# Part of a modulation product in a two-block transformer kernel, moved from VectorE to TensorE

## The chip, the core and the metric

The kernel runs on one core of a Trainium2 chip. The metric is the device time of one execution in microseconds. TensorE is PE in the rows of the profile (its weight loads are listed apart, as PEld), VectorE is DVE, ScalarE is ACT, GpSimd is POOL, and SyncE is SP, which here only starts DMAs.

## What is computed

Two transformer blocks one behind the other, all in fp32. The first has two layers over 256 tokens `x` and 256 context tokens `ctx`, model width 1024. The part that the change touches is the modulation: two vectors, `c` and `c_ctx`, go through silu and a 1024 x 6144 weight, and the six column blocks of 1024 that come out shift, scale and gate everything else in the layer.

```python
def ada_params(cvec, w_ada, b_ada):
    return jnp.split(jax.nn.silu(cvec) @ w_ada + b_ada, N_ADA, axis=-1)

for l in range(DEPTH):                                  # first block, two layers
    sa, ca, ga, sm, cm, gm = ada_params(c_lat, w_ada[l], b_ada[l])
    sa_c, ca_c, ga_c, sm_c, cm_c, gm_c = ada_params(c_cx, w_ada[l], b_ada[l])
    h = modulate(rms_norm(x, g_mix[l]), sa, ca)         # h * (1 + ca) + sa
    ...                                                 # q, k, v, u = h @ w_in
    mix = jnp.concatenate([pool_mixer(u, w_pool[l], s_pool[l]),
                           head_out(o_att, g_subln[l], lam_init)], axis=-1)
    x = x + ga * (mix @ w_out[l])
    x = x + gm * sq_relu_mlp(modulate(rms_norm(x, g_mlp[l]), sm, cm), w_mlp1[l], w_mlp2[l])
    ...                                                 # the same for ctx in layer 0
```

The second block (a block-sparse attention layer, a recurrent layer and two convolutional feed-forwards) follows unchanged and is not touched.

## The kernel before

All large products run on TensorE with the weight in 128 x 128 tiles at rest and 256 tokens moving. Weight and activation are split into a high and a low part (`whi`, `wlo`, `hhi`, `hlo` and so on) and three products of the parts are added up (`unit`, issued from L589). The split costs a cast on ScalarE (L111) and a subtraction on VectorE (L119) for each weight. Weights come in through one stream: SyncE starts the DMAs in the order of the code as buffers come free, three buffers for the raw weights, four for each split part, and a ring of two, `araw`, for the modulation weight.

The program sets the order by hand: each engine executes its instructions in the order of the code, and what stands ahead on an engine's queue and waits holds up what is behind it.

The modulation product is cut into pieces of 256 rows and 512 columns, 512 KB each. For a layer `l`, column block `j` (0 to 5) and half `ch` (0, 1), four pieces `q` make a group. Two of the six column blocks of layer 0 are computed at the start, before anything else; the other pieces stand in a list, (0,2) to (0,5) and then those of layer 1, and are worked off one step at a time. A step is what lies between two `yield`s in `ada_part`. On VectorE (`f`, L270 on) a piece is four instructions, for two row blocks and two vectors, each multiplying the 128 x 512 weight by a scalar per partition and adding to `aacc`: the first two of a group are a plain multiplication (L278), the others a multiply-add (L280). A piece takes two steps, the last of a group three. Then `ada_reduce` transposes `aacc` in 32 x 32 blocks and reduces it, for each vector (L315, L316), and GpSimd adds up the partitions and the bias into `ada` (L319 to L330).

Steps are taken at three kinds of place. In attention, `attend`, the loop over `i` takes `STEPS[l][i]` of them in iteration `i`, behind the filler and ahead of the transposes of the softmax before. In a product, `ada_due` takes some when a quota is due. And `ada_need` takes all that are still missing where a value is used, as in `mod`, which makes the scale `gs` (L532) for the norm ahead of the MLP.

In `attend` of layer 0, 12 items (head, queries) run in 14 iterations. One iteration is: the scores of a later item on TensorE (L983), the row maximum on VectorE (L993, L994), exponentials on ScalarE (L998), the combining step of the item before (L1008), the filler, which is part of a product on TensorE, then reciprocal and scaling of the sum (L1002, L1003), the modulation steps, the transposes of the weights (L1020), and every second or so iteration the product with the values (L1029) whose result is scaled by L1035, L1036 (ScalarE) and L1037 (VectorE). In the last iterations the filler has little left on TensorE; the window sums of the pool mixer run on VectorE (L938 to L945) and its product on TensorE (L954). Behind attention comes the output product `w_out`, whose result goes to the residual `X` (L710), and then the entrance of the MLP: the squares of X are added (`nacc`, L461), `gs` is made, `dhi` (L511) and `dlo` (L513) are the operands of the first products, and further operands follow through L520 to L523.

## Time and profile before

| | us |
|---|---|
| median of 3 runs | 1668.03 |
| lowest and highest run | 1665.22, 1671.71 |
| the profiled execution, its own time | 1664.32 |
| its span in the trace | 1662.4 |
| PE busy | 1558.4 (94%) |
| DVE busy | 1263.0 (76%) |
| ACT busy | 857.4 (52%) |
| POOL busy | 93.4 (6%) |

The mean granted clock of TensorE was 0.963 of full speed. The difference between the profiled execution's own time and its span is what lies before the first and behind the last instruction. The shares are averages over stages that differ. Attention in layer 0 ends with the last pool product, which starts at 206.61 us; the output product follows, and from 290 us on TensorE works on the MLP. A duration in a timeline row is that of the group of instructions in it; two neighbours in the pipeline overlap a little, so the sum of single durations is longer than the stretch.

### The profile page before, as it was taken

Reading aid. Unit: us, or ns where it says so; the run is one execution under the profiler, and the core shown is the slowest. Engines: PE = TensorE matmul, PEld = TensorE weight load, DVE = VectorE, ACT = ScalarE, POOL = GpSimd, SP = SyncE. Lnnn points to the kernel's source line nnn. Section 1 sums busy time; section 2 is a strip of 40 time slices with the busy share of each in tenths; the row PEclk is TensorE's granted clock in tenths of the full one; section 3 lists DMA queues with packets and bytes.
Section 4 is the critical chain, followed back from the end, with each engine's and each line's share of the span. In section 5 each row is a group of like instructions: output and inputs, shape, how many; then the busy total and the mean of one; then the engine's idle time right before and its main releaser. Section 6 shows DMA issues by size and latency. Waiting matters only on the chain.

```text
span 1662.4 us, 31219 instructions
## 1 busy us (share of the span) xinstructions
PE 1558.4 (94%) x12857; PEld 1479.0 (89%) x12857; DVE 1263.0 (76%) x2170; ACT 857.4 (52%) x1460; POOL 93.4 (6%) x238
## 2 busy tenths in 40 slices
PE   7889697999999999797999999899999999899998
PEld 2877497999999999776899999579999998899998
DVE  6889987898876557777966667668886778897673
ACT  5645545522222225765655455536664558776463
POOL 0011000101301001000200000000000000000000
PEclk9899798999999999998999999789999999999999
DMA  9353232454444344443565554215555545455551
GB/s 364 123 148 115 89 124 95 128 182 150 142 149 138 130 152 129 124 148 114 175 234 183 180 172 153 76 50 182 192 180 188 179 153 176 168 182 184 179 193 61
DMA packets 134015, 256.89 MB, mean 155 GB/s; under 512 B 6224, under 2 KB 19184, under 8 KB 132848
## 3 DMA queue, kind: packets, MB, share of 16 engines
q1 hardware_dynamic: 132672, 254.31, 45.8%
q8 instruction: 100, 1.64, 0.4%
q10 hardware_dynamic: 1200, 0.59, 0.1%
q14 instruction: 43, 0.35, 0.1%
HBM read 253.83 MB, written 1.05 MB: 153 GB/s over the span
## 4 chain that ended last, share of the span: by engine, by line
PE 72%; DVE 16%; ACT 8%; issue 2%; DMA 1%; SPq 0%; POOL 0%; DVEq 0%; ACTq 0%; POOLq 0%
PE ps L589 66%; DVE wlo L119 3%; DVE aacc L280 3%; ACT whi L111 1%; DVE m L993 1%; ACT s L918 1%; ACT s L998 1%; DVE X L710 1%; DVE s L938 1%; ACT s L520 1%; DMA raw<-in_w_ada_dram 1%; DVE nacc L461 1%; DVE aacc L315 1%; PE ps L1605 0%; DVE ared L316 0%
## 5 line engine op out<-in xcount | busy, mean ns | idle before, releaser
L111 ACT CAST whi<-raw 128x1024 fp32r<-128x1024 f32 x380 | 393.8, 1047 | 427.1 <-PE ps L589 384.9
L119 DVE TENSOR_TENSOR wlo<-raw,whi 128x1024 fp32r<-128x1024 f32 x380 | 459.0, 1221 | 158.9 <-ACT whi L111 153.8
L589 PE MATMUL ps<-hid,whi 128*128 128x256 f32 x2304 | 295.5, 283 | 0.0
L589 PEld LDWEIGHTS ps<-hid,whi 128*128 128x128 f32 x2304 | 284.8, 192 | 0.0
L280 DVE SCALAR_TENSOR_TENSOR aacc<-araw,cs,aacc 128x512 f32<-128x512 f32 x224 | 157.7, 746 | 11.4 <-DMA araw<-in_w_ada_dram 10.4
L589 PE MATMUL ps<-h2hi,whi 128*128 128x256 f32 x672 | 162.3, 283 | 3.1 <-ACT h2hi L521 3.1
L589 PE MATMUL ps<-h2lo,whi 128*128 128x256 f32 x672 | 162.1, 281 | 0.0
L589 PE MATMUL ps<-hid,wlo 128*128 128x256 f32 x1152 | 156.8, 283 | 0.0
L589 PE MATMUL ps<-fhi,whi 128*128 128x256 f32 x640 | 155.3, 281 | 0.0
L589 PE MATMUL ps<-flo,whi 128*128 128x256 f32 x640 | 155.3, 281 | 0.0
L589 PEld LDWEIGHTS ps<-hid,wlo 128*128 128x128 f32 x1152 | 146.4, 192 | 0.0
L589 PE MATMUL ps<-dhi,whi 128*128 128x256 f32 (+1 forms) x512 | 129.6, 290 | 4.0 <-ACT whi L111 2.1
L589 PEld LDWEIGHTS ps<-h2hi,whi 128*128 128x128 f32 x672 | 128.1, 191 | 3.5 <-ACT h2hi L521 3.5
L589 PEld LDWEIGHTS ps<-h2lo,whi 128*128 128x128 f32 x672 | 127.6, 190 | 0.3 <-DVE h2lo L523 0.3
L589 PE MATMUL ps<-dlo,whi 128*128 128x256 f32 (+1 forms) x512 | 127.4, 285 | 0.2 <-DVE dlo L513 0.2
L589 PEld LDWEIGHTS ps<-fhi,whi 128*128 128x128 f32 x640 | 121.1, 189 | 0.0
L589 PEld LDWEIGHTS ps<-flo,whi 128*128 128x128 f32 x640 | 120.5, 188 | 0.0
L710 DVE SCALAR_TENSOR_TENSOR X<-ps,ada,X 128x256 f32<-128x256 f32 x184 | 75.4, 476 | 39.2 <-PE ps L589 39.2
L589 PEld LDWEIGHTS ps<-dhi,whi 128*128 128x128 f32 x512 | 99.1, 194 | 5.1 <-ACT whi L111 2.3
L589 PEld LDWEIGHTS ps<-dlo,whi 128*128 128x128 f32 x512 | 99.0, 193 | 0.8 <-DVE dlo L513 0.5
L589 PE MATMUL ps<-h2hi,wlo 128*128 128x256 f32 x672 | 89.4, 283 | 0.0
L589 PE MATMUL ps<-fhi,wlo 128*128 128x256 f32 x640 | 89.3, 282 | 0.0
(386 smaller groups left out, 2829.0 us busy)
## 6 DMA issues: line engine op xcount, KB each, us to landing
raw<-in_w_mlp_dram SPq DMA_DIRECT2D x64, 1024.0 KB, 5.4
raw<-in_ffn_w_up_dram SPq DMA_DIRECT2D x48, 1024.0 KB, 5.2
araw<-in_w_ada_dram SPq DMA_DIRECT2D x80, 512.0 KB, 3.8
raw<-in_ffn_w_down_dram SPq DMA_DIRECT2D x24, 1024.0 KB, 5.1
raw<-in_w_in_dram SPq DMA_DIRECT2D x16, 1024.0 KB, 5.6
raw<-in_ev_w_in_dram SPq DMA_DIRECT2D x12, 1024.0 KB, 5.1
raw<-in_w_out_dram SPq DMA_DIRECT2D x8, 1024.0 KB, 5.0
raw<-in_od_w_in_dram SPq DMA_DIRECT2D x8, 1024.0 KB
```

Of the source, the lines that this page charges most:

```text
L111: self.nc.scalar.copy(hi, src)
L119: self.nc.vector.tensor_sub(lo, src, hi)
L280: dve.scalar_tensor_tensor(a[:, v], raw[:, k], c, a[:, v], op0=OP.mult, op1=OP.add)
L315: dve.transpose(a[:, v], a[:, v])
L461: dve.tensor_add(a, a, q)
L520: act.activation(h, src, AF.Identity, bias=sa(n), scale=gs(n))
L589: mm(p, w, x, start=start, stop=stop, skip_group_check=True)
L710: dve.scalar_tensor_tensor(X[:, n, s], b[:, i], gates[s](n), X[:, n, s], op0=OP.mult, op1=OP.add)
L918: act.copy(sw[32 * q:32 * q + 32], src[32 * (q ^ 1):32 * (q ^ 1) + 32])
L938: dve.tensor_add(c[:, :, :width], a[:, :, :width], a[:, :, n:n + width])
L993: dve.reduce_max(m[:, j], banks[j], axis=AX)
L998: act.activation(ei[:, a], banks[j][:, a], AF.Exp, bias=m[:, j, a:a + 1], scale=0.125, accum_out=z[:, j, a:a + 1])
```

## The change

A new function `cols` does a piece on TensorE. For each of four column groups of 128 and two row blocks it makes one fp32 matmul, the raw 128 x 128 weight at rest and the two vectors `cs` moving, two columns, into one bank of 128 x 4 x 2. One VectorE instruction per piece (L322 in the changed code) then adds the eight numbers a partition to the bias, or to `ada` itself. No transposes, no reduces and no GpSimd work follow. A piece is two steps, also at the end of a group. `BY_COLS` sends three groups there: (0,3,0), (0,3,1) and (0,4,0). All other pieces stay with `f`.

```diff
--- before.py
+++ after.py
@@ -236,6 +236,7 @@
     EV_STEPS = (2, 4, 2, 2, 2, 2, 2, 2, 2, 0)
     EV_EVERY = 3
     BY_ROWS = ()
+    BY_COLS = ((0, 3, 0), (0, 3, 1), (0, 4, 0))
     SHIFT_AT = ((1, 6), (8,))
     SHIFT_SEGS = (0, 1)
     MAKE_AT = (4, 0)
@@ -307,7 +308,23 @@
                     done.add((l, j))
             yield True
 
-        return ap, rows if (l, j, ch) in BY_ROWS else f
+        def cols(raw):
+
+            p = bank([128, 4, 2])
+            c0 = 8 * j + 4 * ch
+            for i in range(4):
+                for k in range(2):
+                    mm(p[:, i], raw[:, k, 128 * i:128 * i + 128], cs[:, :, 2 * q + k], start=k == 0, stop=k == 1)
+                if i == 1:
+                    yield False
+            old = pcol("b_ada", 48 * l + c0, 4)[:, None].to_broadcast([128, nv, 4]) if q == 0 \
+                else ada[l][:, :nv, c0:c0 + 4]
+            dve.tensor_add(ada[l][:, :nv, c0:c0 + 4], p.rearrange("p i v -> p v i")[:, :nv], old)
+            if q == 3 and ch == 1:
+                done.add((l, j))
+            yield True
+
+        return ap, cols if (l, j, ch) in BY_COLS else rows if (l, j, ch) in BY_ROWS else f
 
     def ada_reduce(l, j, nv, ch, a):
         red = scr([128, 2, 16], tag="ared", bufs=1)
```

Line numbers move by 1 up to `ada_part` and by 17 behind it; L589 is now L606, L993 is L1010, L1020 is L1037.

TensorE, iteration 7 of attention in layer 0, from the end of the filler (`hlo`, `hhi` are its operands, `s` the softmax, `wT` its transpose). Before:

```order
L589 MATMUL ps<-hlo,whi 128x256
L589 MATMUL ps<-hhi,wlo 128x256 x16
L1020 MATMUL ps<-ident,s 128x128 x4
L1029 MATMUL ps<-wT,v 128x256 x4
L983 MATMUL ps<-kT,qT 128x256 x4
```

With the change:

```order
L606 MATMUL ps<-hlo,whi 128x256
L606 MATMUL ps<-hhi,wlo 128x256 x16
L317 MATMUL ps<-cs,araw 128x2 x16
L1037 MATMUL ps<-ident,s 128x128 x4
L1046 MATMUL ps<-wT,v 128x256 x4
L1000 MATMUL ps<-kT,qT 128x256 x4
```

Sixteen matmuls of two pieces stand between the filler and the transposes.

VectorE, iterations 7 and 8 (`m` is the row maximum, `z` the sums). Before:

```order
L994 TENSOR_SCALAR m_1577<-m_1577 128x2
L1008 SCALAR_TENSOR_TENSOR s<-s,z_1486 128x512
L280 SCALAR_TENSOR_TENSOR aacc<-araw,cs,aacc 128x512 x2
L1002 RECIPROCAL z_1578<-z_1578 128x2
L1003 TENSOR_TENSOR z_1578<-z_1578,nlam_1129 128x1
L280 SCALAR_TENSOR_TENSOR aacc<-araw,cs,aacc 128x512 x6
L993 TENSOR_REDUCE m_1646<-ps 128x2 x2
L994 TENSOR_SCALAR m_1646<-m_1646 128x4
L1008 SCALAR_TENSOR_TENSOR s<-s,z_1578 128x512
L280 SCALAR_TENSOR_TENSOR aacc<-araw,cs,aacc 128x512 x2
```

With the change:

```order
L1011 TENSOR_SCALAR m_1590<-m_1590 128x2
L1025 SCALAR_TENSOR_TENSOR s<-s,z_1511 128x512
L322 TENSOR_TENSOR ada_87<-ps,ada_87 128x2x4
L1019 RECIPROCAL z_1591<-z_1591 128x2
L1020 TENSOR_TENSOR z_1591<-z_1591,nlam_1129 128x1
L322 TENSOR_TENSOR ada_87<-ps,ada_87 128x2x4
L1010 TENSOR_REDUCE m_1671<-ps 128x2 x2
L1011 TENSOR_SCALAR m_1671<-m_1671 128x4
L1025 SCALAR_TENSOR_TENSOR s<-s,z_1591 128x512
L322 TENSOR_TENSOR ada_87<-ps,ada_87 128x2x4
```

Ten multiply-adds are gone from these rows; three adds, which read a bank that TensorE fills, stand in their places, the second of them directly ahead of the next row maximum.

VectorE at the entrance of the MLP, up to `gs` (`nacc_1006` is the sum of squares, `aacc` with its number one group of pieces). Before, where six rows of `nacc` stand in a row and the last two are shown:

```order
L461 TENSOR_TENSOR nacc_1006<-nacc_1006,s1_2486 128x256
L461 TENSOR_TENSOR nacc_1006<-nacc_1006,s1_2489 128x256
L280 SCALAR_TENSOR_TENSOR aacc_2221<-araw_2349,cs_89,aacc_2221 128x512 x4
L315 STREAM_TRANSPOSE aacc_2221<-aacc_2221 128x512
L316 TENSOR_REDUCE ared_2496<-aacc_2221 128x16
L315 STREAM_TRANSPOSE aacc_2221<-aacc_2221 128x512
L316 TENSOR_REDUCE ared_2496<-aacc_2221 128x16
L532 SCALAR_TENSOR_TENSOR gs_2518<-ada0_87,pv_74 128x8
```

With the change:

```order
L119 TENSOR_TENSOR wlo_2438<-raw_1987,whi_2437 128x1024
L332 STREAM_TRANSPOSE aacc_2158<-aacc_2158 128x512
L333 TENSOR_REDUCE ared_2475<-aacc_2158 128x16
L332 STREAM_TRANSPOSE aacc_2158<-aacc_2158 128x512
L333 TENSOR_REDUCE ared_2475<-aacc_2158 128x16
L478 TENSOR_TENSOR nacc_1006<-nacc_1006,s1_2503 128x256
L478 TENSOR_TENSOR nacc_1006<-nacc_1006,s1_2506 128x256
L478 TENSOR_TENSOR nacc_1006<-nacc_1006,s1_2509 128x256
L478 TENSOR_TENSOR nacc_1006<-nacc_1006,s1_2512 128x256
L478 TENSOR_TENSOR nacc_1006<-nacc_1006,s1_2521 128x256
L478 TENSOR_TENSOR nacc_1006<-nacc_1006,s1_2524 128x256
L549 SCALAR_TENSOR_TENSOR gs_2527<-ada0_87,pv_74 128x8
```

The four multiply-adds stand earlier in the program, and the transposes and reduces come ahead of the six rows of `nacc`, not behind them. From `gs` on the order on VectorE is the same in both programs.

## Rows read from the trace of the kernel before

**Rows 1.** Busy time of each engine in five stretches; columns in the first line.

```profile
core 0: us, PE busy (x) PEld busy (x) DVE busy (x) ACT busy (x) POOL busy (x), PEclk, DMA share, GB/s
117.36:167.20 49.84, 44.21 (x287) 35.68 (x287) 46.43 (x89) 28.07 (x64) 6.80 (x24) 0.95 0.34 106
167.20:206.61 39.41, 24.14 (x141) 18.67 (x140) 36.07 (x84) 20.17 (x60) 3.03 (x12) 0.80 0.29 94
206.61:265.00 58.39, 54.89 (x419) 52.71 (x420) 46.71 (x92) 23.26 (x51) 5.18 (x24) 0.96 0.36 119
265.00:290.00 25.00, 18.32 (x107) 16.83 (x108) 19.02 (x44) 18.02 (x38) 0.00 (x0) 0.73 0.25 85
290.00:640.00 350.00, 350.00 (x2935) 350.00 (x2935) 259.70 (x415) 107.20 (x157) 49.43 (x94) 1.00 0.43 145
```

**Rows 2.** The chain of waits from 110 to 300 us, its shares by line.

```profile
by line: PE ps L589 19.3%; DVE aacc L280 16.8%; DVE m L993 7.0%; DVE wlo L119 6.1%; issue 4.4%; ACT s L998 3.8%; DVE s L938 3.8%; DVE ared L316 2.9%; DVE X L710 2.7%; DVE aacc L315 2.7%; ACT s L520 2.6%; DVE s L1008 2.6%; ACT h2hi L521 1.9%
```

**Rows 3.** Timeline of PE: start, length, operation, [idle before it <-releaser].

```profile
123.81 0.63 PE L1020 MATMUL ps<-ident,s 128*128 128x128 f32 x4 [1.52 <-DVE s L1008]
...
143.87 0.63 PE L1020 MATMUL ps<-ident,s 128*128 128x128 f32 x4 [1.94 <-DVE s L1008]
...
157.13 0.63 PE L1020 MATMUL ps<-ident,s 128*128 128x128 f32 x4 [1.87 <-DVE s L1008]
```

**Rows 4.** Instructions on tile aacc: ns min/median/max, first and last start.

```profile
L280 DVE SCALAR_TENSOR_TENSOR aacc<-araw,cs,aacc x224: 735/745/831, 66.6 to 812.0; 128x512 f32<-128x512 f32 x112
L278 DVE TENSOR_SCALAR aacc<-araw,cs x32: 473/481/487, 65.8 to 796.9; 128x512 f32<-128x512 f32 x32
L315 DVE STREAM_TRANSPOSE aacc<-aacc x32: 700/703/715, 84.2 to 814.4; 128x512 f32<-128x512 f32 x32
L316 DVE TENSOR_REDUCE ared<-aacc x32: 685/686/690, 85.0 to 815.2; 128x16 f32<-128x512 f32 x32
```

**Rows 5.** Timelines of DVE and PE at the end of attention.

```profile
195.53 2.73 DVE L280 SCALAR_TENSOR_TENSOR aacc<-araw,cs,aacc 128x512 f32<-128x512 f32 x4
...
206.61 2.08 PE L954 MATMUL ps<-uT,wpool 128*128 128x512 f32 x2 [7.89 <-ACT uT L947]
```

**Rows 6.** Timeline of PEld, last sums; group of PE on L851, transposes.

```profile
1653.78 0.97 PEld L1980 LDWEIGHTS ps<-ones,nacc 128*128 128x128 f32 x8
1654.67 0.97 PEld L1980 LDWEIGHTS ps<-ones,s 128*128 128x128 f32 x8
...
L851 PE MATMUL ps<-ident,arow x16: 197/198/222, 41.5 to 42.5; 4*128 4x4 f32 x16
```

**Rows 7.** Timelines of DVE, ACT and PE ahead of the MLP.

```profile
245.53 1.41 DVE L280 SCALAR_TENSOR_TENSOR aacc<-araw,cs,aacc 128x512 f32<-128x512 f32 x2
246.85 2.10 DVE L461 TENSOR_TENSOR nacc<-nacc,s 128x256 f32<-128x256 f32 x6
248.87 2.73 DVE L280 SCALAR_TENSOR_TENSOR aacc<-araw,cs,aacc 128x512 f32<-128x512 f32 x4
...
257.28 0.17 DVE L532 SCALAR_TENSOR_TENSOR gs<-ada,pv 128x8 f32<-128x8 f32 x1 [2.93 <-POOL ada L330]
...
257.48 1.71 ACT L511 ACTIVATE dhi<-X,gs 128x256 fp32r<-128x256 f32 x4 [12.39 <-DVE gs L532]
...
264.83 0.39 PE L589 MATMUL ps<-dhi,whi 128*128 128x258 f32 x1 [2.11 <-ACT whi L111]
```

**Rows 8.** Timelines of ACT and DVE, iteration 5, the head's scaling.

```profile
138.78 0.46 ACT L1035 ACTIVATE s<-ps,eps 128x256 f32<-128x256 f32 x1
...
140.29 0.48 DVE L1037 SCALAR_TENSOR_TENSOR s<-ps,gsub,s 128x256 f32<-128x256 f32 x1
```

**Rows 9.** The page's DMA issues: count, KB each, us to landing.

```profile
araw<-in_w_ada_dram SPq DMA_DIRECT2D x80, 512.0 KB, 3.8
```

**Rows 10.** Busy time, columns as in rows 1, during and behind small matmuls.

```profile
1096.00:1100.00 4.00, 2.18 (x192) 2.02 (x179) 3.40 (x9) 1.17 (x3) 0.00 (x0) 0.87 0.02 4
1100.00:1104.00 4.00, 4.00 (x73) 2.30 (x75) 2.15 (x8) 1.47 (x5) 0.00 (x0) 0.50 0.02 4
```

## The prediction

> **What bounds the kernel now.** I read first the busy time of the engines in five stretches of layer 0 [rows 1]. The twelve pieces lie in attention (117.36 to 206.61 us) and in the output product behind it (to 265). From 290 on TensorE is busy 350.00 of 350 us, so whatever leaves VectorE there gains nothing that shows. What counts is how early TensorE reaches that point.
>
> Then the chain of waits from 110 to 300 us, summed by line [rows 2]. The multiply-adds (L280) stand second with 16.8% of 190 us; with their reduces and transposes the old product is 22% of the chain. VectorE's work is not hidden there, and that speaks for the change. But in the first stretch TensorE is itself busy 44.21 of 49.84 us; 5.63 are free on it, in four waits of one line, three of them shown in [rows 3]. The chain leaves VectorE there only to meet an engine that is nearly full. In the second stretch TensorE works 24.14 of 39.41 us: there is room.
>
> **What is removed.** A group of four pieces is 2 TENSOR_SCALAR, 14 multiply-adds, 2 transposes and 2 reduces on VectorE. By the medians [rows 4] that is 2 x 0.481 + 14 x 0.745 + 2 x 0.703 + 2 x 0.686 = 14.2 us a group, 42.5 for three; neighbours overlap (four multiply-adds take 2.73, so 0.68 each [rows 5]), which makes 39.7 of VectorE's time. By the order of before, 26 multiply-adds, 4 TENSOR_SCALAR and one set of transposes and reduces are in the first stretch (22.4), and 10, 2 and one set in the second (10.5). GpSimd's sums behind the reduces go too.
>
> **What is added: 96 fp32 matmuls**, each with a 128x128 weight and two moving columns. The nearest rows are the last sums of the kernel, weight 128x128, fp32, one column [rows 6]: four matmuls (eight records) from 1653.78 to 1654.67, 0.89 us, so 0.222 each. I take this value: weight, type and narrow moving side are the same. 96 x 0.222 = 21.3 us. From below: 16 transposes whose weight is 128 columns on 4 partitions start between 41.5 and 42.5, 0.067 each, 6.4 us in all. From above: twice the first, 0.444, if the clock is granted at half, 42.6. By order, 72 stand in the first stretch (iterations 2 to 8), 20 in the second (iterations 9 and 10), 4 in the output product. There are also 12 adds on VectorE, of 8 elements a partition, as `gs` has (0.17 [rows 7]).
>
> The Trainium skill, "TensorE: Matmul & The Clock Gate", section "Back-to-back issue gap", gives about 25 ns as the floor between matmuls of 1 to 64 columns; an estimate by it is 192 records x 25 ns = 4.8 us, and all of it would vanish in the idle time. The same page, section "LDWEIGHTS (loading the stationary operand)", has the number of weight columns over 1.2 per ns, 107 ns for 128, an estimate of 20.5 us. The 0.111 us per record of [rows 6] sides with the second.
>
> **First stretch.** 72 x 0.222 = 16.0 us more for TensorE. The waits for the weighted softmax (1.52, 1.94 and 1.87 [rows 3], the fourth being the rest of the 5.63) should vanish, since VectorE has 22 us less to do. New waits: (1) An iteration's multiply-adds ran beside TensorE's filler product; now the tensor_add (L322 of the changed code) stands ahead of the next row maximum (L993) and waits for matmuls that TensorE issues after the filler. Queued behind it on VectorE are that maximum, then the exponentials on ScalarE, and through them the next iteration's transposes. VectorE has little else to do and TensorE has the next filler, so I cost it at nothing; without that cover it is about 2 us for each of seven iterations, as in [rows 3]. (2) The scores of iterations 5 and 7 take a bank whose last reader is the head's scaling on VectorE (L1037 of before); its chain from ScalarE's Ln at 138.78 to 140.77 is 2.0 us [rows 8], of which I see some 0.8 uncovered each: 1.6. (3) In iteration 7 the matmuls of two pieces stand in a row. The ring `araw` has two buffers, so the DMA of the second is issued when the piece two places ahead has been read, 8 matmuls (1.78 us) before its turn, and lands in 3.8 us [rows 9]: 2.0. Together 3.6. Stretch: 16.0 - 5.6 + 3.6 = **+14.0**. Bounds: -5.6 + 4.8 = -0.8 with matmuls of 0.067 and no new wait; +28 with wait (1) in all seven.
>
> **Second stretch.** VectorE, busy 36.07 of 39.41 us, loses 10.5 and gets five adds (0.8): -9.7 if it alone sets the end. TensorE gains 20 x 0.222 = 4.4, twelve ahead of iteration 9's transposes and eight ahead of iteration 10's, through which the next row maximum comes; I count three quarters, +3.2. The pool product that ends the stretch waited 7.89 us for the window sums [rows 5], which stay. I take **-6.5**; bounds 0 and -9.7.
>
> **Output product.** TensorE is busy 54.89 of 58.39 us; four matmuls, **+0.9** (1.8 at half clock).
>
> **Entrance to the MLP.** The groups have 8 steps instead of 9, so each later piece comes up to three steps earlier. Before, two multiply-adds, six nacc adds, four multiply-adds, two transposes and two reduces stood ahead of `gs`; now the transposes and reduces come first, then the six adds. By [rows 7], 1.41 + 2.73 of multiply-adds are gone from this place, and the 2.93 that `gs` waited for GpSimd's sums is covered by the adds (2.10): 6.2, less some 0.1 of overlap at each seam, 5.8. ScalarE stood 12.39 us for `gs`, so it gets all of that. TensorE's first wait here, 2.11, is for a weight that ScalarE casts behind those operands, and it is idle 25.00 - 18.32 = 6.7 us in all to 290. **-5.8**; bounds 0 (TensorE's own end of the output product, 2.11 us ahead of 264.83, frees the last weight buffers) and -6.7.
>
> **Sum.** 14.0 - 6.5 + 0.9 - 5.8 = +2.6; with half of one fall of the clock in iteration 7 (half of 2.0, rival A) about +3 or 4. The profiled run took 1664.32 us (span 1662.4, and 1.9 around it), 3.7 below the median of 1668.03; a run like it would now take some 1667.5, and the median **1671 us**. A measurement of this kernel can tell about 0.5%, 8.3 us, from no change.
>
> **Rivals.** (A) The clock. Where 192 records of small matmuls stood in 4 us, TensorE busy 2.18 of it, the granted clock was 0.87, and in the next 4 us 0.50, its lower level (1.2 of 2.4 GHz), though TensorE was then busy throughout [rows 10]. Blocks of 12 and 16 matmuls that move two columns may do the same to attention. A fall that holds for 4 us costs 2.0 of them. It decides from three falls on: 2.6 + 6.0 = 8.6; four to six give +11 to +15, 1679 to 1683. For it: the second stretch already has a clock of 0.80. Against: the new blocks take 0.9 to 3.6 us and lie between wide matmuls, and the idle times that stood in those places, up to 1.94, left 0.95 in the first stretch.
> The Trainium skill, the same page, section "HAM oscillation — how this bites in real kernels", tells of short bursts with waits between them that each start cold; no row here has such a block inside attention.
> (B) The entrance gives nothing: `gs` comes earlier, but TensorE waits for weights as before. 2.6 + 5.8 = +8.4, 1676.4, on the bound. For it: TensorE's first wait there names the cast of a weight, not `gs`. Against: ScalarE's 12.39 us, with the weight casts behind it in its queue.
> (C) The new matmuls cost 0.067 as at L851: first stretch 4.8 - 5.6 + 3.6 = +2.8, second -9.7 + 1.0, output product +0.3, entrance -5.8: -11.4, 1657. For it: two columns are little work. Against: [rows 6].
> That the product does not move is excluded by the order: 42 multiply-adds are gone.
>
> **How the numbers follow.** Forecast 0.52, nearly all within 0.5%; A 0.22, nearly all slower; B 0.13, half on either side of the bound; C 0.13, faster. So faster 0.13, same 0.59, slower 0.28. The forecast's own terms, the second stretch and the entrance above all, can be off by 6 to either side. The range 1658 to 1682 reaches to C below and to most of A above and leaves out about one in ten at each end.
>
> **What would show it.** Right: a group L317 with 0.11 us a record on the weight side; the first stretch 14 us longer, TensorE busy in 95% of it; the second 6 us shorter; `gs` some 6 us nearer to the end of the output product, and the rest shifted as a whole. Wrong: a granted clock below 0.85 in iterations 2 to 8 (A); still 25 us between the end of the output product and a full TensorE (B); L317 records that start 0.03 to 0.07 apart (C); TensorE idle ahead of the transposes while VectorE waits with an add ahead of the row maximum, which is the wait (1) that I left at nothing.

## The result and the profile after

The changed kernel takes longer. In the first comparison its median is 1685.16 us (1683.38 to 1685.83, 4 runs) against 1666.73 (1665.22 to 1671.71, 4 runs): ratio 1.0101, 95% interval 1.0073 to 1.0128. A later comparison, with 4 and 23 runs, gave 1684.01 against 1671.89: 1.0081, 1.0056 to 1.0105. The forecast of 1671 us is missed and so is its upper end, 1682. The profiled execution took 1683.38 us with a span of 1681.7, 19.3 us more span than before.

The four stretches of layer 0, busy time of each engine, columns in the first line. The first two begin and end at the same instructions as in [rows 1], the scores of iterations 2 and 9 and the last pool product; the third is cut at TensorE's end of the output product, the fourth at the point from which TensorE is full:

```profile
core 0: us, PE busy (x) PEld busy (x) DVE busy (x) ACT busy (x) POOL busy (x), PEclk, DMA share, GB/s
116.57:187.56 70.99, 68.44 (x431) 58.18 (x431) 30.44 (x72) 30.08 (x66) 2.85 (x12) 0.84 0.29 89
187.56:223.20 35.64, 26.95 (x181) 22.30 (x180) 22.59 (x62) 18.80 (x57) 0.00 (x0) 0.87 0.27 90
223.20:279.76 56.56, 55.17 (x424) 53.17 (x425) 43.22 (x88) 26.09 (x56) 2.97 (x12) 0.96 0.36 114
279.76:299.73 19.97, 13.05 (x104) 12.52 (x102) 15.01 (x37) 13.06 (x29) 0.00 (x0) 0.99 0.31 106
```

They last 70.99, 35.64, 56.56 and 19.97 us. Before, cut at the same instructions, they were 49.84, 39.41, 55.78 and 25.38, the last two by these rows of before:

```profile
206.61:262.39 55.78, 54.39 (x416) 52.39 (x417) 44.77 (x87) 20.65 (x46) 5.18 (x24) 0.96 0.35 116
262.39:287.77 25.38, 16.59 (x104) 15.46 (x103) 19.76 (x47) 18.46 (x39) 0.00 (x0) 0.77 0.31 104
```

So +21.2, -3.8, +0.8 and -5.4, 12.8 in all. As 0.8 had been gained ahead of iteration 2, the MLP, from which on TensorE is full, is reached 12 us later (299.73 against 287.77). TensorE is busy 68.44 of 70.99 us in the first stretch where 44.21 of 49.84 were before, and its granted clock there is 0.84 in place of 0.95. VectorE, busy 46.43 us there before, is down to 30.44. Some 7 us of the 19.3 were lost far behind the change. Of these, 5.1 were lost in the second block, between 1044 and 1179 us (below), and 2.0 in the 742 us between the MLP and 1030 us of before. That distance is 740.7 to 744.3 us in the kernels of the experiments, so no cause is given for the 2.0. The forecast had the time within 0.5%; it moved by 0.8 to 1.0%.

The chain of waits over the same work, 110 to 312 us, by line, beside [rows 2]:

```profile
by line: PE ps L606 36.4%; PE ps L317 8.9%; PE ps L1000 5.9%; PE ps L1046 5.7%; DVE wlo L119 2.9%; PE ps L1037 2.9%; issue 2.9%; DVE X L727 2.5%; ACT s L537 2.5%; DVE s L955 2.5%; DVE aacc L281 2.0%; ACT h2hi L538 1.8%; DMA araw<-in_w_ada_d
```

The multiply-adds (L281 here) went from 16.8% to 2.0%, and TensorE took their place: the big products (L606) went from 19.3% to 36.4%, the new matmuls (L317) have 8.9%, scores and values (L1000, L1046) 5.9 and 5.7%. The wait was not removed, it changed its owner.

The new matmuls as a group, then TensorE in iterations 6 and 7 of attention (start, length, operation, idle before it and what ended that):

```profile
L317 PEld LDWEIGHTS ps<-cs,araw x192: 187/192/333, 121.1 to 228.4; 128*128 128x128 f32 x192
L317 PE MATMUL ps<-cs,araw x192: 165/251/352, 121.3 to 228.4; 128*128 128x2 f32 x192
```

```profile
154.77 2.74 PE L317 MATMUL ps<-cs,araw 128*128 128x2 f32 x24
157.88 0.60 PE L1037 MATMUL ps<-ident,s 128*128 128x128 f32 x4
158.41 0.70 PE L1000 MATMUL ps<-kT,qT 64*128 64x256 f32 x2
159.58 2.07 PE L1000 MATMUL ps<-kT,qT 64*128 64x256 f32 x6 [0.47 <-DVE s L1054]
...
161.96 0.41 PE L606 MATMUL ps<-hlo,whi 128*128 128x256 f32 x1
162.17 0.41 PE L606 MATMUL ps<-hhi,whi 128*128 128x256 f32 x1
...
166.63 2.73 PE L317 MATMUL ps<-cs,araw 128*128 128x2 f32 x24
171.39 1.83 PE L317 MATMUL ps<-cs,araw 128*128 128x2 f32 x8 [2.03 <-DMA araw<-in_w_ada_dram]
```

Twelve matmuls are 24 records, two each, and take 2.74 us, so 0.11 us a record. Single durations are longer (192 and 251 ns), since they overlap. After them come the scores, three quarters of which waited 0.47 us for the head's scaling; then filler at 0.21 us from start to start (161.96, 162.17), where it takes 0.12 at full clock. The granted clock from 162 to 164 us is 0.50, the lower level. The block of 16 matmuls is split by the wait of 2.03 us for a DMA.

The entrance to the MLP on VectorE, beside [rows 7]:

```profile
265.04 0.69 DVE L333 TENSOR_REDUCE ared<-aacc 128x16 f32<-128x512 f32 x1
265.64 2.24 DVE L478 TENSOR_TENSOR nacc<-nacc,s 128x256 f32<-128x256 f32 x6
269.23 0.17 DVE L549 SCALAR_TENSOR_TENSOR gs<-ada,pv 128x8 f32<-128x8 f32 x1 [1.34 <-POOL ada L347]
```

No multiply-adds stand ahead of `gs` any more, and it waits 1.34 us for GpSimd instead of 2.93.

### The profile page after: what moved, and what is told of

Read it like the earlier page. It is cut to its first block, busy times and chain, and to the rows that moved or that the text cites. A ratio compares the mean times of both kernels' runs of the same rounds, so it can differ in the third digit from the quotient of the medians.

```text
span 1681.7 us, 31510 instructions
## 1 busy us (share of the span) xinstructions
PE 1585.8 (94%) x13049; PEld 1506.1 (90%) x13049; DVE 1227.0 (73%) x2122; ACT 858.0 (51%) x1460; POOL 83.1 (5%) x202
## 4 chain that ended last, share of the span: by engine, by line
PE 75%; DVE 12%; ACT 8%; issue 2%; DMA 1%; POOL 0%; DVEq 0%; SPq 0%; ACTq 0%; POOLq 0%
PE ps L606 67%; DVE wlo L119 3%; ACT whi L111 1%; ACT s L935 1%; PE ps L317 1%; DVE aacc L281 1%; PE ps L1046 1%; PE ps L1000 1%; DVE m L1010 1%; DMA araw<-in_w_ada_dram 1%; ACT s L537 1%; DVE X L727 1%; DVE s L955 1%; DMA raw<-in_w_ada_dram 1%; ACT s L1015 1%
## 5 line engine op out<-in xcount | busy, mean ns | idle before, releaser
L606 PE MATMUL ps<-hid,whi 128*128 128x256 f32 x2304 | 295.5, 283 | 0.0
L606 PEld LDWEIGHTS ps<-hid,whi 128*128 128x128 f32 x2304 | 284.8, 192 | 0.0
L606 PE MATMUL ps<-h2hi,whi 128*128 128x256 f32 x672 | 162.5, 283 | 5.0 <-ACT h2hi L538 5.0
L606 PE MATMUL ps<-h2lo,whi 128*128 128x256 f32 x672 | 162.2, 282 | 0.0
L606 PE MATMUL ps<-hid,wlo 128*128 128x256 f32 x1152 | 156.8, 283 | 0.0
L606 PE MATMUL ps<-flo,whi 128*128 128x256 f32 x640 | 155.3, 281 | 0.0
L606 PE MATMUL ps<-fhi,whi 128*128 128x256 f32 x640 | 155.3, 281 | 0.0
L606 PEld LDWEIGHTS ps<-hid,wlo 128*128 128x128 f32 x1152 | 146.4, 192 | 0.0
L281 DVE SCALAR_TENSOR_TENSOR aacc<-araw,cs,aacc 128x512 f32<-128x512 f32 x182 | 128.6, 745 | 10.4 <-DMA araw<-in_w_ada_dram 9.6
L606 PEld LDWEIGHTS ps<-h2hi,whi 128*128 128x128 f32 x672 | 128.4, 191 | 5.4 <-ACT h2hi L538 5.4
L606 PE MATMUL ps<-dhi,whi 128*128 128x256 f32 (+1 forms) x512 | 128.2, 288 | 1.9 <-DVE pv L439 1.9
L606 PEld LDWEIGHTS ps<-h2lo,whi 128*128 128x128 f32 x672 | 127.7, 190 | 0.3 <-DVE h2lo L540 0.3
L606 PE MATMUL ps<-dlo,whi 128*128 128x256 f32 (+1 forms) x512 | 126.7, 284 | 0.8 <-DVE dlo L530 0.8
L606 PEld LDWEIGHTS ps<-fhi,whi 128*128 128x128 f32 x640 | 121.1, 189 | 0.0
L606 PEld LDWEIGHTS ps<-flo,whi 128*128 128x128 f32 x640 | 120.5, 188 | 0.0
L606 PEld LDWEIGHTS ps<-dhi,whi 128*128 128x128 f32 x512 | 98.3, 192 | 2.6 <-DVE pv L439 2.1
L606 PEld LDWEIGHTS ps<-dlo,whi 128*128 128x128 f32 x512 | 98.4, 192 | 1.2 <-DVE dlo L530 1.0
L606 PE MATMUL ps<-h2hi,wlo 128*128 128x256 f32 x672 | 89.6, 283 | 0.0
L606 PE MATMUL ps<-fhi,wlo 128*128 128x256 f32 x640 | 89.3, 282 | 0.0
```

Of the source, the lines that this page charges most:

```text
L281: dve.scalar_tensor_tensor(a[:, v], raw[:, k], c, a[:, v], op0=OP.mult, op1=OP.add)
L606: mm(p, w, x, start=start, stop=stop, skip_group_check=True)
```

## The experiments

Lengths of stretches below are cut at the same four instructions in each kernel.

**Does the clock fall because the new matmuls move so little?** Only the number of moving columns is changed:

```diff
-            p = bank([128, 4, 2])
+            p = bank([128, 4, 64, 2])
...
-                    mm(p[:, i], raw[:, k, ...], cs[:, :, 2 * q + k], start=k == 0, stop=k == 1)
+                    mm(p[:, i], raw[:, k, ...], cs[:, None, :, 2 * q + k].to_broadcast([128, 64, 2]), ...)
```

> The changed kernel with 128 moving columns in place of 2 in each of the 96 matmuls (the two vectors repeated 64 times; the add reads the first pair). The number of instructions is the same. Theory (idle array): iterations 2 to 8 of attention took 21 us more than before where 14 were worked out, because the granted clock was at its lower level for 17 us more, behind the blocks of narrow matmuls; with 128 columns, a moving time of about half the 0.111 us that a weight load takes in the trace, the matmuls cost the same and the clock stays up. Then the stretch of iterations 2 to 8 gets 5 to 7 us shorter, at a granted clock of 0.93 or more in place of 0.81, and the kernel takes 1678 to 1681. Rival (waits): the clock fell for the 2.1 us and 2.0 us waits (for the head's scaling, and for a DMA), whatever the matmuls move; then the clock stays near 0.81 and the kernel near 1685. Second rival (columns cost): moving 128 fp32 columns adds to each matmul, 0.05 us a record, and the stretch gets longer by up to 7 us.

It took 1678.79 us (6 runs), inside the expected 1678 to 1681, against 1667.29 (21 runs), ratio 1.0069 (1.0044 to 1.0095). The stretches, then TensorE in iteration 7:

```profile
116.60:182.70 66.10, 62.61 (x433) 53.20 (x432) 30.52 (x73) 30.18 (x68) 2.85 (x12) 0.95 0.32 95
182.70:216.81 34.11, 25.42 (x182) 21.38 (x181) 22.69 (x62) 18.77 (x57) 0.00 (x0) 0.93 0.29 95
216.81:273.70 56.89, 55.50 (x425) 53.51 (x426) 43.24 (x88) 26.08 (x56) 2.96 (x12) 0.95 0.35 114
273.70:293.67 19.97, 13.07 (x105) 12.53 (x103) 15.01 (x37) 13.05 (x29) 0.00 (x0) 1.00 0.31 106
```

```profile
158.37 1.13 PE L1001 MATMUL ps<-kT,qT 64*128 64x256 f32 x6 [0.47 <-DVE s L1055]
...
159.78 0.28 PE L607 MATMUL ps<-hhi,whi 128*128 128x256 f32 x1
159.90 0.28 PE L607 MATMUL ps<-hlo,whi 128*128 128x256 f32 x1
...
167.32 1.85 PE L317 MATMUL ps<-cs,araw 128*128 128x128 f32 x8 [2.09 <-DMA araw<-in_w_ada_dram]
```

The clock in iteration 7: the filler in the changed kernel, then the same filler and the stretch behind the DMA wait with 128 columns (columns as above):

```profile
162.00:164.00 2.00, 2.00 (x11) 2.00 (x11) 0.47 (x1) 1.30 (x4) 0.00 (x0) 0.50 0.00 0
```

```profile
160.00:162.00 2.00, 2.00 (x19) 2.00 (x18) 1.23 (x3) 1.35 (x4) 0.00 (x0) 1.00 0.00 0
168.00:170.00 2.00, 2.00 (x11) 2.00 (x11) 0.00 (x0) 0.00 (x0) 0.00 (x0) 0.50 0.41 158
```

With 64 times the moving columns the same 144 records of the first stretch take 18.6 us of TensorE where they took 17.8, some of those at the lower clock; the granted clock of the first stretch is 0.95 again, as before the change, and the stretch is 66.10 us instead of 70.99, the second 34.11 instead of 35.64. The filler starts 0.12 apart, and the waits of 2.09 us for the DMA and 0.47 for the head's scaling are still there. In time at the lower level, (1 - 0.84) x 2 x 70.99 = 23 us with two columns, and (1 - 0.95) x 2 x 66.10 = 7 with 128.

Cut into steps of 1 us, the stretch begins in both kernels, and in before, with some 3 to 5 us at the lower level. Behind that the changed kernel has three more spells, of 3.4, 6.8 and 6.8 us, around 127, 163 and 173 us. With 128 columns one is left, 3.4 us, right behind the wait for the DMA. So with the same waits most of the falls go with the two columns, and the waits account at most for the one that is left. Three profiles with two columns have 0.84 in this stretch (the changed kernel twice, and once with shifted code), one with 128 has 0.95. A fall is not bound to the new matmuls, though: the second profile of before has one spell of 3.4 us more than the first, at a clock of 0.92, and is as long.

The rival that columns cost is out. As whole times the kernels with 2 and with 128 columns lie close (1.0073 to 1.0128 and 1.0056 to 1.0105 against 1.0044 to 1.0095); the gain is read from the traces, where the MLP is reached at 293.67 instead of 299.73 us.

**What do the matmuls cost as such?** One matmul in a piece, with eight columns, the rest left out:

```diff
-                for k in range(2):
-                    mm(p[:, i], raw[:, k, 128 * i:128 * i + 128], cs[:, :, 2 * q + k], ...)
+                if i == 0:
+                    mm(p, raw[:, 0, 0:128], cs[:, 0], start=True, stop=True)
```

> The changed kernel with one matmul a piece in place of eight (one 128x128 weight, eight columns): 7/8 of the product is left out, and the order, the waits, the adds on VectorE and the DMAs stay. It tells what the 84 missing matmuls cost. Theory: iterations 2 to 8 lose 63 matmuls of 0.222, 14.0 us, and the lower clock that came with them, some 7, and the second stretch 17 matmuls, 3.8: the MLP is reached 17 to 25 us earlier than in the changed kernel, 5 to 13 earlier than in before. Rival (the waits that the change adds, VectorE's add ahead of the row maximum and the DMA ring, cost most of it): the MLP is reached less than 12 us earlier than in the changed kernel.

One run took 1654.15 us. Its stretches:

```profile
116.70:169.60 52.90, 49.54 (x305) 39.46 (x304) 29.44 (x69) 30.13 (x68) 2.84 (x12) 0.90 0.39 123
169.60:202.13 32.53, 23.35 (x147) 18.40 (x147) 23.49 (x66) 18.55 (x57) 0.00 (x0) 0.89 0.31 108
202.13:257.10 54.97, 53.58 (x416) 51.58 (x417) 43.13 (x88) 26.07 (x56) 2.96 (x12) 0.97 0.34 108
257.10:277.07 19.97, 13.10 (x104) 12.56 (x102) 15.02 (x37) 13.07 (x29) 0.00 (x0) 1.00 0.32 105
```

The MLP is reached at 277.07, 22.7 us earlier than in the changed kernel and 10.7 earlier than before: inside both ranges of the theory. The 84 matmuls are 84 x 0.222 = 18.6 of the 22.7. The other 4.1 is less than what the clock gave back with 128 columns (4.9 + 1.5), and the clock of the first stretch is 0.90 here and not 0.95. So with nearly all of the product gone from TensorE, the change brings about 11 us up to the MLP, 5.4 of them at the entrance. The first stretch is 52.90 all the same, 3 longer than before. In it are 2.9 us of the matmuls that are left and a new wait of 2.6 us for the exponentials, with 6.8 us at the lower clock behind it; whether a free product would shorten this stretch is not shown.

**Is the entrance's gain that of the order alone?** The kernel before, with one step less at a group's end:

```diff
-                if k == 0 or q == 3:
+                if k == 0 or q == 3 and (l, j, ch) not in ((0, 3, 0), (0, 3, 1), (0, 4, 0)):
                     yield False
```

> The kernel before, with only the number of steps changed: in the three groups (0,3,0), (0,3,1), (0,4,0) the last piece is two steps and not three, as in the change, and the multiply-adds stay on VectorE. So later pieces come up to three steps earlier, and at the entrance to the MLP two transposes and two reduces stand ahead of the six sums of squares, with no multiply-adds behind those. Theory: the entrance's gain (5.4 us from the end of the output product to the first MLP product, in the changed kernel) comes from that place alone; then it is here too, 4 to 6 us, attention is as before within 2 us, and the kernel takes 1661 to 1664. Rival: it needs VectorE free of the old product; then the multiply-adds, which now press together ahead of the entrance, lengthen attention or the output product by as much as the entrance gives, 1665 to 1670.

1671.21 us (10 runs) against 1671.29 (25 runs), ratio 1.0009 (0.9989 to 1.0030): no difference, where 1661 to 1664 was expected.

```profile
116.20:168.20 52.00, 44.68 (x288) 35.34 (x287) 46.84 (x91) 26.72 (x64) 7.07 (x24) 0.94 0.32 102
168.20:210.87 42.67, 24.61 (x141) 20.05 (x140) 38.81 (x88) 21.68 (x62) 7.46 (x12) 0.80 0.31 99
210.87:266.20 55.33, 53.94 (x417) 51.94 (x418) 46.84 (x94) 26.00 (x56) 7.52 (x24) 0.97 0.37 117
266.20:286.15 19.95, 13.05 (x104) 12.51 (x103) 14.99 (x37) 13.04 (x29) 0.00 (x0) 1.00 0.32 106
```

The entrance is 19.95 us, as in the changed kernel, and 5.4 less than before: the place of the steps alone gives it. But attention pays for it, 52.00 and 42.67 us instead of 49.84 and 39.41, with VectorE busier in both. This is the rival's case: the work moved ahead costs there what it gave behind.

**One group only**, (0,4,0), for which TensorE has room:

```diff
-    BY_COLS = ((0, 3, 0), (0, 3, 1), (0, 4, 0))
+    BY_COLS = ((0, 4, 0),)
```

> The changed kernel with one group, (0,4,0), by matmuls instead of three; (0,3,0) and (0,3,1) go by VectorE as before. Its 32 matmuls fall into the second stretch, iterations 9 to 12, where TensorE worked 24 of 39 us before. Theory (TensorE is full in the first stretch and has room in the second): iterations 2 to 8 as before within 1 us; the second stretch shorter by 3 to 6 us; the entrance to the MLP shorter by 2 to 5 us, since the following group comes one step earlier and not three; against it 128 instructions more, half a block of code, which by the fetch theory costs 5 to 8 us in the second block. Sum 1660 to 1668. Rival (no room): the matmuls stand on the chain in the second stretch too, which stays as long as before or gets longer by up to 7 us; then 1672 to 1680.

1672.95 us (10 runs) against 1667.29 (21 runs), ratio 1.0020 (0.9998 to 1.0041). First and second stretch:

```profile
117.70:169.60 51.90, 47.40 (x287) 37.91 (x286) 48.30 (x91) 30.07 (x66) 6.79 (x24) 0.88 0.34 102
169.60:204.89 35.29, 25.99 (x181) 21.75 (x181) 28.53 (x75) 18.55 (x57) 3.03 (x12) 0.96 0.33 105
```

The second stretch is 4.1 us shorter, as expected; the output product is 58.21 and the entrance 24.04 (55.78 and 25.38 before), and the first stretch 51.90, though no new matmul is in it. Its clock was 0.88, with the lower level behind a wait of 2.6 us for the exponentials, which before does not have, and behind one of 1.9 us; why it differs there is open. The MLP is reached 0.6 us earlier than before, and the second block gives that back (below). Of what was expected only the second stretch came; the total lies where the rival had it, for another reason.

**The roles swapped**: the vectors at rest, the weight moving, on a path that stands unused in the kernel. It is brought to two steps a piece as well (that part of the edit is left out here).

```diff
-    BY_ROWS = ()
-    BY_COLS = ((0, 3, 0), (0, 3, 1), (0, 4, 0))
+    BY_ROWS = ((0, 3, 0), (0, 3, 1), (0, 4, 0))
+    BY_COLS = ()
...
```

> The same twelve pieces on TensorE the other way round: the two vectors at rest and the raw weight moving, 512 columns (a path that stands unused in the kernel), two matmuls a piece, and once a group a copy on ScalarE, four small transposes and one add; two steps a piece, as in the change. Price: 24 matmuls of 512 moving fp32 columns, two records each; the scores, of that shape, take four records in 1.07 us, so 0.53 a matmul, 12.8 us in place of 21.3, and 12 transposes at 0.067. Theory (idle array): these move 512 columns and keep the clock; iterations 2 to 8 hold 18 of them, 9.6 less the 5.6 of waits: +4, the second stretch -7, the entrance -5, so the MLP is reached 6 to 9 us earlier than in before, at a granted clock of 0.9 or more in iterations 2 to 8. 120 instructions more shift the code by nearly half a block, worth 0 to 7 us in the second block: 1659 to 1668. Rival (the scalar copies and transposes at the end of a group stand on the chain, and a DMA for the ring is late as before): the MLP is reached later than in before, 1670 or more.

1681.21 us (10 runs) against 1671.29 (25 runs), ratio 1.0060 (1.0040 to 1.0079). The group of its matmuls, and three of them in iteration 6:

```profile
L294 PEld LDWEIGHTS ps<-araw,cs x48: 81/84/85, 121.0 to 224.9; 128*2 128x2 f32 x48
L294 PE MATMUL ps<-araw,cs x48: 592/592/1061, 121.0 to 225.7; 128*2 128x512 f32 x48
...
154.60 2.74 PE L294 MATMUL ps<-araw,cs 128*2 128x512 f32 x6
```

The clock stayed up (0.94 in the first stretch), but the price was wrong: six records take 2.74 us, so 0.91 us a matmul, not the 0.53 taken from the scores, and 24 of them come to 22 us, as much as 96 the other way. The scores were no fit row; why they are cheaper was not tried (their weight has 64 partitions and 128 columns, this one 128 and 2). The MLP is reached 11 us later than before, not 6 to 9 us earlier.

**Where do the 5 us in the second block come from?** The page of before counts 100 fetches of the instruction queue and 1.64 MB, so 16 KB a fetch, for 25,714 instructions of TensorE: an estimate of some 256 instructions a fetch, called a block here. The 96 new matmuls are 384 instructions, one and a half blocks. Four kernels only shift the code, with tiny matmuls at the start: before with 32, 64 or 12 of them (128, 256, 48 instructions), and the changed kernel with 32, which makes two whole blocks:

```diff
     apv = [bank([128, 512]) for _ in range(4)]
+    for _ in range(32):
+        mm(apv[0][:32, 0:2], ones[:32, :32], ones[:32, 0:2], start=True, stop=True)
```

> The kernel before with 32 tiny fp32 matmuls (32x32 weight, two columns) ahead of its first transpose, where TensorE waits 2.68 us for a DMA anyway; they write a bank that is overwritten later. Nothing else is changed. In the trace 96 new matmuls of the change are 192 matmul and 192 weight-load records, 384 instructions; the instruction queue (q8) fetches 16 KB at a time, 100 times in before, for some 25,700 instructions of TensorE, so some 256 instructions a fetch: the change moves all later fetches by one and a half blocks, and 32 matmuls (128 instructions) move them by half a block. Theory (fetch): in the second block's chunk stage, between 1067 and 1120 us, TensorE stood 1.8 us without instructions before and 5.9 us after; it is the place of the block boundaries against a 1 MB transfer there that cost the change 6.9 us of its 18. Then this kernel, with the boundaries of the changed one and none of its work, loses 5 to 8 us in that stage, 1672 to 1675 us, and up to layer 0's MLP it runs as before, within 1 us. Rival (lateness): the stage lost because it was reached 12 us later, in another position against the clock and the transfers; then this kernel takes as long as before, within 2 us.

> The changed kernel with the same 32 tiny matmuls at the start: 512 instructions more than before, two whole blocks, so the boundaries of the fetches stand where they stood before. Theory (fetch): the 5.9 us without instructions go back to about 2 and the kernel gains 5 to 8 us, to 1677 to 1680; layer 0 stays 12 us longer than before. Rival (lateness): as the changed kernel, 1685 within 2.

> The control for the half block of code: the kernel before with 64 tiny matmuls at the start instead of 32, 256 instructions, one whole fetch of 16 KB, so the boundaries of the fetches stand where they stood before. With 32, all ten runs took 1669.9 to 1675.6 us, where half of those of before lie at 1662.6 to 1669. Theory (code position): with 64 the lower runs come back, at least three of ten below 1669, and the longest stall without instructions in the second block is 2 us or less. Rival (the small matmuls at the start, or chance): no run of ten below 1669, as with 32.

> The kernel before with 12 tiny matmuls at the start, 48 instructions, a fifth of a block. In the stretch that was 1030 to 1160 us in before, TensorE stood idle 12.3, 12.5, 12.6, 12.6, 12.3 us in the five kernels whose code is shifted by 128 instructions (half a block), 11.0 with 120, but 8.5, 9.2, 9.7, 8.3, 9.6, 8.1 in six with a whole number of blocks, and 7.0 in the one shifted by 48, whose longest stall without instructions was 0.3. Theory (code position): this kernel, shifted by 48 with no other change, stands 6.3 to 7.7 us idle there, with no stall for instructions over 0.5 us, and takes about 1 to 2 us less than before; layer 0 is as before. Rival (the 7.0 came from the missing work and the earlier time): 8 to 10 us idle, as in before.

The stretch from 1030 to 1160 us of before, cut at the same instructions, in before, the changed kernel, before with half a block, before with a whole one; columns as above:

```profile
1030.00:1160.00 130.00, 121.45 (x1492) 98.50 (x1491) 94.44 (x195) 69.89 (x149) 0.00 (x0) 0.87 0.29 99
```

```profile
1044.00:1179.10 135.10, 122.78 (x1492) 99.33 (x1491) 94.41 (x195) 69.92 (x149) 0.00 (x0) 0.86 0.29 95
```

```profile
1031.20:1170.90 139.70, 127.15 (x1490) 102.13 (x1490) 94.40 (x195) 69.80 (x149) 0.00 (x0) 0.82 0.29 92
```

```profile
1029.90:1168.40 138.50, 128.80 (x1491) 103.05 (x1490) 94.30 (x195) 69.84 (x149) 0.00 (x0) 0.82 0.29 93
```

Length less busy time is TensorE's idle time: 8.6, 12.3, 12.6 and 9.7 us. The fetches in the changed kernel (count, MB, share):

```profile
q8 instruction: 102, 1.67, 0.4%
```

Waits for nothing but the next instruction, in before and in the changed kernel (engine, line, what it waited for; total, times, longest):

```profile
PE ps L1605 <- issue: 1.8, 1, 1.8
```

```profile
PE ps L1622 <- issue: 5.9, 2, 3.7
```

In the kernels whose code is shifted by half a block, or by one and a half, the idle time is 12.3 (after), 12.5 (after once more), 12.6 (before with half a block), 12.6 (128 columns) and 12.3 (one group); with a whole number of blocks it is 8.6 and 9.2 (before, twice), 9.7, 8.3 (the changed kernel brought to a whole block), 9.6 (steps only) and 8.1 (the mixture below). On average 12.5 against 8.9: the place of the code costs 3.5 us. The stall for instructions moves with it: 5.5 to 5.9 us in the first five, 1.8 to 3.7 in the other six. The busy time in the same stretch is a second thing: 118.4 to 128.8 us at a clock of 0.91 to 0.82, and it does not follow the code: 127.2 with half a block, 128.8 with a whole.

In times: before with half a block 1671.23 (10 runs, none under 1669.86; 1672 to 1675 was expected) against 1667.29, ratio 1.0023 (1.0005 to 1.0041), with a whole block 1673.37 against 1671.89, 1.0010 (0.9992 to 1.0029), two of ten under 1669 where three were expected; the changed kernel brought to a whole block 1683.23 (4 runs), 1.0092, where 1677 to 1680 was expected. So the stall is shown in the traces, and in the times it is not: the intervals with half a block and with a whole one overlap, and the changed kernel gained 1 to 2 us and not 5 to 8. What this stage takes varies by more than that. With a fifth of a block the stall comes to 1.4 us, 0.6 at most in one piece, but a wait of 1.1 us for VectorE is new, and TensorE stood idle 9.2 us in that trace, as the rival had it, not the 6.3 to 7.7 expected; it took 1664.82 (12 runs) against 1669.62 (17 runs), 0.9983 (0.9966 to 1.0001).

**Both kernels once more.**

> The kernel before, once more. Its 21 runs of the first comparison fall into two heaps, 1663 to 1667 and 1672 to 1675. Theory (chance): the second block's chunk stage, small matmuls that move few columns, takes one of two times, some 7 us apart, by where the clock falls and code arrives, from execution to execution; layer 0 is the same in all. Then these runs show both heaps again, and a profile from the upper one has its 7 us between 1067 and 1150 us and none up to there. Rival: the two heaps are of chips or of whole executions; then the difference is spread over the kernel.

> The changed kernel once more, for its time beside more runs of before (before: 1662.6 to 1675.9 in 25 runs, median 1671.3; the changed kernel so far 1683.4 to 1685.8 in 4). Theory: the change costs 12 us in layer 0 in every execution, and the rest of the measured 18 was how few runs fell in the second block; then the medians differ by 12 to 16 us here, and the stretches of layer 0 repeat within 1 us: 71 for iterations 2 to 8, 36, 57, 20. Rival: 18 again, so that 6 of it belong to the change.

Before: 1670.31 us (10 runs, 1663.29 to 1674.20). Its profile has the same stretches in layer 0 within 0.4 us (49.84, 39.39, 55.37, 25.36) and 2.4 us more in the second block's stage, 1.7 of it busy time: so part of the spread sits there. But the ten times do not fall into two heaps (1663.3, four from 1666.8 to 1669.4, five from 1671.2 to 1674.2), and the profile came from the second lowest, so where the upper runs lose their time was not seen. The changed kernel: 1684.01 us, 12.1 over the median of before beside it, the low end of the theory's 12 to 16; its stretches repeat within 1.1 us, 72.10, 35.72, 56.38, 19.99, and the clock of the first is 0.84 again.

**The mixture that the runs pointed to**: one group by wide matmuls, two steps for the other two, code brought to a whole block.

> What the runs so far point to: group (0,4,0) alone by matmuls, with 128 moving columns; (0,3,0) and (0,3,1) on VectorE but with two steps at the end, so that the entrance to the MLP has no multiply-adds ahead of the scale; 32 tiny matmuls at the start, which with the 128 instructions of the group make a whole block of code. From the stretches measured: iterations 2 to 8 52 us (49.8 before), the second 35 to 38 (39.4), the output product 57 (55.8), the entrance 20.0 (25.4): 164 to 167 in place of 170.4. Theory: 3 to 6 us less than before. Rival: the multiply-adds pressed ahead lengthen the second stretch by 3 as with steps alone and the product holds the bank of the pool mixer; then as before within 2 us.

1672.56 us (12 runs) against 1671.89 (23 runs), ratio 1.0012 (0.9995 to 1.0028).

```profile
117.60:171.10 53.50, 47.64 (x303) 38.48 (x302) 48.62 (x92) 28.66 (x65) 7.07 (x24) 0.92 0.33 101
171.10:213.71 42.61, 28.84 (x182) 24.31 (x181) 28.46 (x74) 19.65 (x59) 6.13 (x12) 0.85 0.30 97
213.71:270.10 56.39, 55.00 (x424) 53.00 (x425) 43.18 (x88) 26.04 (x56) 2.96 (x12) 0.96 0.37 115
270.10:290.12 20.02, 13.11 (x104) 12.57 (x102) 15.07 (x37) 13.10 (x29) 0.00 (x0) 0.99 0.32 106
```

The entrance is 20.02 us, but the second stretch 42.61, as with the steps alone (42.67), though VectorE is down to 28.46 us there: the gain of one group does not add to that of the steps. This is the rival. The trace shows what the stretch lost:

```profile
177.73 0.16 DVE L323 TENSOR_TENSOR ada<-ps,pv 128x8 f32<-128x8 f32 x1
178.04 0.55 PE L607 MATMUL ps<-hhi,whi 128*128 128x256 f32 x1 [4.89 <-DVE ada L323]
```

TensorE's filler waits 4.89 us for the add of the first piece. That add empties the bank of the new matmuls, which were through at 170.3 us, and stands on VectorE behind a group's transposes and reduces, three subtractions for weights and a window sum. Behind this wait the granted clock is 0.50 from 178 to 182 us. No version beats the kernel before by more than its interval.

## Why the prediction was wrong, point by point

**What bounds.** Right that the first stretch would leave VectorE only to meet a full TensorE: 70.99 us long, it has 2.55 us of idle TensorE.

**The price of a matmul.** Right at full clock, 0.11 us a record; but L317 takes 17.8 us in the first stretch where 16.0 was summed, part of it at the lower clock. It is not the columns that set the price, since 128 cost nearly as much as two (18.6 us). Rival C is out; of the two figures of the Trainium skill, "TensorE: Matmul & The Clock Gate", weighed there, the 107 ns of "LDWEIGHTS (loading the stationary operand)" stands near the 111 measured, the 25 ns of "Back-to-back issue gap", a floor given there without the weight load, does not.

**The first stretch: the step that failed.** +14.0 was summed, +21.2 came. The waits went nearly as worked out: the 5.63 us vanished, the DMA wait in iteration 7 was put at 2.0 and measured at 2.03, the head's scaling cost 0.47 once (0.8 twice was assumed), and no wait of TensorE for the add ahead of the row maximum shows. But busy time was 44.21 + 16.0 = 60.2 by the sum and 68.44 in the trace. The term that failed is the clock: the sum took the clock of before as unchanged and put a fall at half of 2.0, about 1 us, as a rival with a chance of 0.22. The runs showed 23 us of this stretch at the lower level. With 128 columns the stretch gets 4.9 us shorter and 62.6 of busy time are left; the other 2.3 of the 7.2 is about the price of the records, 18.6 us there against 16.0. Rival A was the case in the first stretch, by the mechanism written there, and its sign, a granted clock below 0.85, came with 0.84. Its argument against, that the idle times of before had not lowered the clock, looked at idle times where it should have looked at narrow matmuls. That the +12 at the MLP lies in its +11 to +15 is in part luck, since the second stretch and the price of the records are in it too.

**The second stretch.** -6.5 taken, -3.8 measured, within the bounds of 0 and -9.7; with the clock kept up it is -5.3.

**Output product and entrance.** +0.9 and -5.8 taken, +0.8 and -5.4 measured. The mechanism of the entrance was right too: it is the order of the steps, which the run with steps alone gives without any matmul. What the prediction did not see is that the same order has a price in attention when VectorE keeps its work.

**The sum** to the MLP was +2.6 and came out at +12. The first stretch brought 7.2 of the difference, the second 2.7, the entrance 0.4; 0.8 had been gained ahead of them.

**Behind the MLP.** "The rest shifted as a whole" failed: the second block's stage got 5.1 us longer. 384 instructions move the code behind them by one and a half blocks of 16 KB, and TensorE then stands 5.9 us without instructions among the matmuls of 32x32, where it stood 1.8 before. No term of the sum held that. By the idle times (12.3 against 8.6) it is 3.8 of the 5.1; the other 1.3 is busy time. Part of the measured 18 us was also which runs of before stood beside: the first four have a median of 1666.73, later ones of 21, 25, 23 and 17 runs have 1667.29, 1671.29, 1671.89 and 1669.62.

## What to carry to other kernels

Moving work from an engine that is on the chain to one that is 89% busy (44.21 of 49.84 us) pays only if the work costs less there than the free time; here 16 us of new matmuls met 5.6 of free time. A matmul with a 128x128 weight at rest cost here with two columns what it cost with 128, and blocks of it with two columns were followed by the lower clock for the wide matmuls behind them; if such a block must be, try repeating the moving columns, which cost almost nothing here (2.85 us in place of 2.74 for 24 records). And an order of steps can be tried apart from the arithmetic that it comes with: the 5.4 us at the MLP were the order's, not the change's.

## What the runs showed of the hardware that was not expected

- 96 fp32 matmuls with a 128x128 weight take 0.11 us a record at full clock with 2 moving columns and with 128; with 2 the granted clock of the first stretch is 0.84, with 128 it is 0.95.
- Swapping the roles gives nothing in fp32: two columns at rest and 512 moving take 0.46 us a record, 0.91 a matmul, so 22 us for the same product.
- The position of the code matters: 128 instructions of no use at the start of the program, in time that was idle, changed TensorE's idle time 1,030 us later from 8.6 to 12.6 us, where it runs through hundreds of matmuls of 32x32; 256 instructions left it at 9.7.
